# A transformer block with 32 experts: tokens 64 to 96 of an expert in banks of their own, the rarer rest at the end, the first expert without a branch

## The chip, the cores and the metric

The kernel runs on one core of one Trainium2 chip. The metric is device time in microseconds (us) from launch to end. Before the change it is 1229.9 us, the median of three runs (1229.08 to 1230.4).

Names: PE is the matrix engine, PEld its weight loads, DVE the vector engine, ACT the scalar engine, POOL GpSimd, SP the engine that issues the weight transfers. An engine's sequencer, which takes its branches and register loads, has the same name with a q behind it (PEq; PEldq in listings by line).

## The reference

x has 256 tokens of 1024 features. Attention and its merge come first; the change does not touch them. Behind them a router picks 4 of 32 experts for each token, and the experts are added up:

```python
def moe_ffn(h, w_router, b_router, w_gate_up, b_gate_up, w_down, b_down):
    hf = h.reshape(b * s, d)
    logits = (hf @ w_router + b_router).astype(jnp.float32)
    top_val, top_idx = lax.top_k(logits, TOP_K)            # TOP_K = 4
    top_w = jax.nn.softmax(top_val, axis=-1)
    combine = jnp.sum(jax.nn.one_hot(top_idx, N_EXPERTS) * top_w[..., None], axis=1)
    y = jnp.zeros_like(hf)
    for e in range(N_EXPERTS):                             # 32
        gu = hf @ w_gate_up[e] + b_gate_up[e]              # 1024 -> 2048
        gate = jnp.minimum(gu[:, :D_EXPERT], SWIGLU_LIMIT)
        up = jnp.clip(gu[:, D_EXPERT:], -SWIGLU_LIMIT, SWIGLU_LIMIT)
        act = (up + 1.0) * (gate * jax.nn.sigmoid(SWIGLU_ALPHA * gate))
        y = y + combine[:, e:e + 1] * (act @ w_down[e] + b_down[e])   # 1024 -> 1024
```

The result goes through an RMS norm, a gate and the residual: `x + gt_f * rms_norm(ffn_out, g_post_ffn)`. All is float32, so an expert has 12.58 MB of weights.

## The kernel before

The first 240 us or so are the mixing part and the router. Then the expert phase runs over all 32 experts in order, and all weights of all experts are read once.

**The weight stream.** An expert's weights are six pieces of 2 MB: four quarters of `w_gate_up[e]` and two halves of `w_down[e]`. `Slots.pump` (L76) puts them on SP's queue in one fixed order, the halves of `w_down[e-1]` behind the quarters of `w_gate_up[e]`. Ten slots of the on-chip memory take turns. The transfer into a slot waits until PE has read the piece that lay there.

**A step.** Step j multiplies the up product of expert j and the down product of expert j−1. A gather (L922, `gather_quad`, every fourth step, for four experts) collects the first 64 tokens of an expert as columns. The up product (`up_mm`, L959) is 64 matmuls of 64 rows by 512 columns into two banks, `ps_g`. ACT and DVE copy one bank each to memory (`up_out`, L972 and L970). Then come, on PE, on odd steps the scatter of the two experts before (`add_pair`, L1072, 8 matmuls into the four banks `y`) and the rows for the next scatter (L1061), and on all steps two times 16 matmuls of `down(j-1)` (L1026), each half followed by four transposes of the copied up product (`up_act`, L979). DVE and ACT add the biases, clip and apply the sigmoid to the transposes (L986 to L998), and take the down product out of its bank (`down`, L1048 on ACT and L1049 on DVE).

**The arms.** An expert can have more than 64 tokens. `counts` (L875 to L883) counts the tokens of each expert and writes a number `arm[j]` per step. Each step begins with `more(j)`: all engines load `arm[j]` (L1132) and branch (L1133) over code that does tokens 64 to 96, 96 to 128, 128 to 192 and 192 to 256 (`CHUNKS`) of expert j−1 (down, `more_down`) and expert j (up, `more_up`). The up product of an arm uses the same two banks `ps_g`. `hint(j)` tells PE beforehand where the branch will go. In these inputs expert 11 alone has over 64 tokens, and not over 96: its arm runs ahead of step 11 (up) and ahead of step 12 (down).

**The order around the branches.** A scheduler sorts each engine's instructions by their data; code of an arm and code outside do not mix, so that an instruction stands ahead of a branch or behind it. `add_pair` had no place of its own: one of its matmuls stands ahead of the odd step's up product, seven behind it. `more(E)`, the branch after the last step, covers the arm of expert 31. Behind it comes the end: the broadcast of a row by PE (`ps_bc`, L292), the rest of `down(31)`, the last scatter, the norm's root, which ACT forms by two functions (L227 and L228) for each half of the tokens, the last DVE operation (L1214) with the residual x, which SP reloads (L1204), and the write of the output. `preload_act_table_set(EXP_LN)` (L1198) loads ACT's function table for the root ahead of that branch.

## Time and profile before

| what | us |
|---|---|
| median of three runs | 1229.9 (1229.08 to 1230.4) |
| the profiled execution | 1233.0 |
| its span, first to last instruction | 1231.3 |
| PE busy in the span | 1090.5 (89%) |
| DVE busy | 441.0 (36%) |
| ACT busy | 247.5 (20%) |
| weight queue, share of the 16 DMA engines | 90.5%, 459.87 MB |
| mean granted PE clock | 0.943 |

All sums are made within the profiled execution, so against its span of 1231.3 us and not against the median. PE and the DMA engines are both near 90% on the average of the span. An average can't say which of them limits a stretch, so stretches are read one by one below. In a timeline the bracket at the end of a row is the idle time of the engine before the row's instruction and what ended it. DMA share 1.00 means that all 16 engines were busy all the time.

### The profile page before, as it was taken

The page shows a single profiled execution, that of the slowest core. Times are in us where ns is not written, and L with a number is a line of the kernel's source. Part 1 is how long each engine was busy: PE and PEld are TensorE (multiplying, and loading weights), DVE is VectorE, ACT ScalarE, POOL GpSimd, SP SyncE. Part 2 cuts the span into 40 slices and gives each one's busy share as a digit, 9 for nine tenths or more (in the row PEclk, how much of TensorE's full clock was granted, in tenths as well). Part 3 has the DMA queues.
Part 4 walks back from the last instruction along what each step waited for, and adds up shares of the span by engine and source line. Part 5 has one row for each costly group of instructions (what it writes and reads, how often), then busy time and mean ns, then how long its engine had stood idle before and what let it go on. Part 6 is the DMA issues. An engine that isn't in the chain of part 4 may idle for free. (4 is left out here: it accounts for less than half of the span.)

```text
span 1231.3 us, 14468 instructions
## 1 busy us (share of the span) xinstructions
PE 1090.5 (89%) x5655; PEld 543.4 (44%) x5655; DVE 441.0 (36%) x952; ACT 247.5 (20%) x473; POOL 30.3 (2%) x44
## 2 busy tenths in 40 slices
PE   4999999688798898998979998998998989989997
PEld 3987899533243334334333333334333423343333
DVE  2587977522222323222132223223233232232224
ACT  2355774520011101001110011101101110010013
POOL 2022000200000000000000000000000000000000
PEclk9999999788899989888989999999999999999999
DMA  9978796768999999999559999999999999999992
GB/s 301 392 273 332 285 402 260 306 257 337 426 374 385 426 426 426 422 426 427 237 228 419 424 426 428 424 426 427 426 425 427 424 426 427 426 426 427 425 397 96
DMA packets 52357, 464.09 MB, mean 377 GB/s; under 512 B 4149, under 2 KB 4266, under 8 KB 27498
## 3 DMA queue, kind: packets, MB, share of 16 engines
q1 hardware_dynamic: 51274, 459.87, 90.5%
q8 instruction: 85, 1.39, 0.5%
q0 software_dynamic: 352, 0.67, 0.4%
q10 hardware_dynamic: 576, 1.57, 0.3%
q14 instruction: 70, 0.57, 0.1%
HBM read 460.01 MB, written 2.10 MB: 375 GB/s over the span
## 5 line engine op out<-in xcount | busy, mean ns | idle before, releaser
L959 PE MATMUL ps_g<-w,xe 128*64 128x512 f32 (+1 forms) x2112 | 501.0, 642 | 76.1 <-ACTq L1133 59.7
L959 PEld LDWEIGHTS ps_g<-w,xe 128*64 128x64 f32 (+1 forms) x2112 | 168.2, 146 | 387.7 <-issue 308.6
L1026 PE MATMUL ps_d<-w,act 128*64 128x512 f32 x992 | 226.0, 597 | 2.2 <-ACT xe L903 2.2
L970 DVE COPY gu<-ps_g 128x512 f32<-128x512 f32 x32 | 22.1, 692 | 438.5 <-PE ps_g L959 438.5
L1026 PEld LDWEIGHTS ps_d<-w,act 128*64 128x64 f32 x992 | 69.0, 137 | 121.8 <-issue 112.8
L972 ACT COPY gu<-ps_g 128x512 f32<-128x512 f32 x33 | 19.3, 585 | 492.1 <-PE ps_g L959 492.1
L463 PE MATMUL ps_p<-hT,whi 128*128 128x256 f32 x512 | 97.0, 290 | 3.2 <-ACT whi L412 3.2
L986 DVE TENSOR_TENSOR gate<-ps_t,bcol 128x256 f32<-128x256 f32 x64 | 27.2, 424 | 165.1 <-PE ps_t L979 116.0
L463 PEld LDWEIGHTS ps_p<-hT,whi 128*128 128x128 f32 x512 | 80.5, 194 | 6.7 <-ACT whi L412 3.5
L413 DVE TENSOR_TENSOR wlo<-w,whi 128x1024 fp32r<-128x1024 f32 x56 | 68.5, 1227 | 29.9 <-ACT whi L412 29.4
L463 PE MATMUL ps_p<-hT,wlo 128*128 128x256 f32 x256 | 72.8, 288 | 0.3 <-DVE wlo L413 0.2
L995 ACT ACTIVATE act<-gate 128x256 f32<-128x256 f32 x64 | 26.6, 416 | 219.1 <-DVE gate L994 219.1
L412 ACT CAST whi<-w 128x1024 fp32r<-128x1024 f32 x56 | 58.5, 1047 | 58.6 <-PE ps_p L463 27.9
L979 PEld LDWEIGHTS ps_t<-ident,gu 128*128 128x128 f32 x260 | 36.3, 209 | 53.1 <-issue 50.3
L1048 ACT ACTIVATE dn<-ps_d,wsl 64x512 fp32r<-64x512 f32 x62 | 42.3, 682 | 82.6 <-PE ps_d L1026 67.0
L922 PE MATMUL ps_x<-p,xn 128*128 128x256 f32 (+1 forms) x288 | 43.1, 304 | 10.7 <-DVE cf L880 4.4
L463 PEld LDWEIGHTS ps_p<-hT,wlo 128*128 128x128 f32 x256 | 49.0, 193 | 1.7 <-DVE wlo L413 1.4
L979 PE MATMUL ps_t<-ident,gu 128*128 128x128 f32 x260 | 48.7, 310 | 0.9 <-ACT gu L972 0.8
L1072 PE MATMUL y<-dn,st 128*128 128x512 f32 x128 | 38.1, 420 | 12.4 <-PEq L1133 9.5
L922 PEld LDWEIGHTS ps_x<-p,xn 128*128 128x128 f32 x288 | 40.9, 218 | 14.5 <-issue 6.2
L1049 DVE SCALAR_TENSOR_TENSOR dn<-ps_d,wsl,dn 64x512 fp32r<-64x512 f32 x62 | 46.4, 748 | 1.5
L1072 PEld LDWEIGHTS y<-dn,st 128*128 128x128 f32 x128 | 22.8, 188 | 31.9 <-issue 22.1
(248 smaller groups left out, 777.3 us busy)
## 6 DMA issues: line engine op xcount, KB each, us to landing
w<-in_w_gate_up_dram SPq DMA_DIRECT2D x128, 2048.0 KB, 18.5
w<-in_w_down_dram SPq DMA_DIRECT2D x62, 2048.0 KB, 16.2
w<-in_w_in_dram SPq DMA_DIRECT2D x8, 2048.0 KB, 8.0
w<-in_w_mod_dram SPq DMA_DIRECT2D x8, 2048.0 KB, 10.1
w<-in_w_mod_dram SPq DMA_DIRECT2D x4, 1024.0 KB, 8.6
w<-in_w_mod_dram SPq DMA_DIRECT2D x8, 512.0 KB
w<-in_w_in_dram SPq DMA_DIRECT2D x8, 512.0 KB, 11.5
w<-in_w_out_dram SPq DMA_DIRECT2D x2, 2048.0 KB
```

Source lines behind the costliest of these rows:

```text
L412: nc.scalar.copy(hi, w)
L413: nc.vector.tensor_tensor(lo, w, hi.bitcast(FT), op=OP.subtract)
L463: mm(ps[:, f % 2, :], w[:, kk, f * 128:(f + 1) * 128], hT[:, a, k, :], start=(k == 0 and i == 0 and f % 2 == 0), stop=(k == NK - 1 and i = ...
L922: mm(px[:, j, :], xn[:, t, a, feature(k0 + j)], p[:, t].rearrange("p a b -> p (a b)"), start=(t == 0 and a == 0), stop=(t == 1 and a == 1))
L959: last = mm(pg[b][s * C:(s + 1) * C, :], xe[:, k, :], wt[:, k % 2, c0:c0 + 512], start=(k == 0), stop=(k == NK - 1), skip_group_check=True)
L979: nc.tensor.transpose(pt[:, j, :], gu[:, j:j + 509:4], ident)
L986: nc.vector.tensor_tensor(dst, pt[:, :, 64 * m:64 * m + 64], bcol[:, b0 + 4 * b:b0 + 4 * b + 4, None].to_broadcast([128, 4, 64]), op=OP.add)
L995: state_act["sig"] = nc.scalar.activation(sig, gate, AF.Sigmoid, scale=1.702)
L1026: mm(pds[h][p0:p0 + C, :], a, wt[:, k % 4, h * 512:(h + 1) * 512], start=(k == 0), stop=(k == NK - 1), skip_group_check=True)
L1048: state_act["down"] = nc.scalar.activation(hi, pds[h][rows, :], AF.Copy, scale=weight)
L1049: nc.vector.scalar_tensor_tensor(lo, pds[h][rows, :], weight, hi.bitcast(FT), op0=OP.mult, op1=OP.subtract)
L1072: mm(yps[t][h], sts[p][:, h, t * 128:(t + 1) * 128], dns[p][:, h, a, :], start=False, stop=False, skip_group_check=True)
```

## The change

- The arms in the steps do tokens 64 to 96 only. Their up product goes to a bank `ps_go` of the pool that the transposes use. A dummy transpose into each of the two banks `ps_g` (L1118) at the beginning of the arm makes PE the engine that last used them.
- Tokens from 96 on (for expert 0: from 64 on) are done behind the last step, in `more(E)`, by `rest`, chunk by chunk under branches on a new table `cnt`, with weights that POOL reloads into the slots (`Slots.again`). `arm[E]` holds 4 more when one of them is needed.
- `more(0)` is gone. `counts` stands behind the first up product instead of ahead of the first gather.
- `add_pair` is placed behind the end of the up product.
- The hint for the last branch goes to ACT and DVE too.
- The preload of ACT's table is tied to the last down and sigmoid ahead of `more(E)`.
- The zero fill `aov` and the copies of activations to memory (`aov_far`) are gone.

```diff
@@ -79,6 +79,11 @@
     def data(self, name, slot, shape, dt=FT):
         assert self.ready(name, slot), name
         return self.pools[slot].tile(shape, dt, name=name, tag=f"w{slot}")
+
+    def again(self, i, slot):
+        src, shape, _, _ = self.items[i]
+        self.tiles[i] = self.pools[slot].tile([128] + list(shape), FT, name=f"w{slot}", tag=f"w{slot}")
+        self.nc.gpsimd.dma_start(self.tiles[i], src)
 
     def done(self, *names):
         self.gone.update(names)
@@ -207,6 +212,7 @@
     comb = keep.tile([128, 2, E], FT, name="comb")
     rank = keep.tile([128, 2, E], FT, name="rank")
     arm = keep.tile([1, E + 1], I32, name="arm")
+    cnt = keep.tile([1, E], I32, name="cnt")
     rs = keep.tile([128, 2], FT, name="rs")
     m8 = keep.tile([128, 2, 8], FT, name="m8")
     oh = keep.tile([128, 2, TOPK, E], FT, name="oh")
@@ -857,8 +863,6 @@
     mk = ctx.enter_context(tc.tile_pool(name="moe", bufs=1, side="right"))
     wk = ctx.enter_context(tc.tile_pool(name="ework", bufs=1, side="right"))
     aov = mk.tile([128, 256], FT, name="aov")
-    nc.gpsimd.memset(aov, 0.0)
-    aov_far = dram.tile([128, 1280], FT, name="aov_far")
     rp = mk
     bd = wk.tile([2 * E, 512], FT, name="bd", tag="st_e")
     for h in range(2):
@@ -870,17 +874,21 @@
 
     def counts():
 
+
         pn = pst.tile([1, E], FT, name="ps_n", tag="t")
         for t in range(2):
             mm(pn, ones[:, 0:1], msk[:, t, :], start=(t == 0), stop=(t == 1))
-        cf = wk.tile([1, 2, E + 2], FT, name="cf", tag="so")
-        cm = wk.tile([1, 2, E + 1], FT, name="cm", tag="pwt")
+        cf = wk.tile([1, 3, E + 2], FT, name="cf", tag="so")
         nc.vector.memset(cf, 0.0)
-        nc.vector.tensor_scalar(cf[:, 0, 1:E + 1], pn, 64.0, None, op0=OP.is_gt)
-        nc.vector.tensor_scalar(cf[:, 1, 1:E + 1], pn, 96.0, 3.0, op0=OP.is_gt, op1=OP.mult)
-        nc.vector.scalar_tensor_tensor(cm[:, 0, :], cf[:, 0, 0:E + 1], 2.0, cf[:, 0, 1:E + 2], op0=OP.mult, op1=OP.add)
-        nc.vector.tensor_tensor(cm[:, 1, :], cf[:, 1, 0:E + 1], cf[:, 1, 1:E + 2], op=OP.max)
-        nc.vector.tensor_tensor(arm, cm[:, 0, :], cm[:, 1, :], op=OP.max)
+        nc.vector.tensor_copy(cnt, pn)
+        nc.vector.tensor_scalar(cf[:, 0, 2:E + 1], pn[:, 1:E], 64.0, None, op0=OP.is_gt)
+        nc.vector.scalar_tensor_tensor(cf[:, 1, 0:E + 1], cf[:, 0, 0:E + 1], 2.0, cf[:, 0, 1:E + 2], op0=OP.mult,
+                                       op1=OP.add)
+        nc.vector.tensor_scalar(cf[:, 2, 0:1], pn[:, 0:1], 64.0, 4.0, op0=OP.is_gt, op1=OP.mult)
+        nc.vector.tensor_scalar(cf[:, 2, 1:E], pn[:, 1:E], 96.0, 4.0, op0=OP.is_gt, op1=OP.mult)
+        nc.vector.tensor_reduce(cf[:, 2, E:E + 1], cf[:, 2, 0:E], AX.X, OP.max)
+        nc.vector.tensor_tensor(cf[:, 1, E:E + 1], cf[:, 1, E:E + 1], cf[:, 2, E:E + 1], op=OP.add)
+        nc.vector.tensor_copy(arm, cf[:, 1, 0:E + 1])
 
     def weights():
 
@@ -960,6 +968,7 @@
                               start=(k == 0), stop=(k == NK - 1), skip_group_check=True)
                     if k == ks[0]:
                         state_act["up"] = last
+                    state_act["up_end"] = last
             if release and k % 2:
                 W.done(i_gu[e][k // 2])
         return pg
@@ -967,9 +976,9 @@
     def up_out(pg, b, tag, bufs):
         gu = wk.tile([128, 512], FT, name="gu", tag=tag, bufs=bufs)
         if b % 2:
-            nc.vector.tensor_copy(gu, pg[b])
+            state_act["evac_dve"] = nc.vector.tensor_copy(gu, pg[b])
         else:
-            nc.scalar.copy(gu, pg[b])
+            state_act["evac_act"] = nc.scalar.copy(gu, pg[b])
         return gu
 
     def up_act(e, C, b, gu, act):
@@ -1097,52 +1106,62 @@
                 mm(yps[t][h], ct[h * E:(h + 1) * E, t * 128:(t + 1) * 128], bd[h * E:(h + 1) * E, :], start=True,
                    stop=False, skip_group_check=True)
 
-    def chunk_act(i, write):
+    ov = aov.rearrange("p (j m) -> p j m", m=64)
+
+    def more_down(e):
+        s0, C = CHUNKS[0]
+        scatter(down_32(e, ov, "guo"), scatter_rows(e, s0, "so", C))
+
+    def more_up(e):
+        s0, C = CHUNKS[0]
+        for bank in gu_banks():
+            nc.tensor.transpose(bank[:, :128], ident, ident)
+        xo = gather([e], s0, C, "xo")[:, :, 0, :]
+        pg = up_mm(e, C, xo, pg=[pst.tile([128, 512], FT, name="ps_go", tag="t")])
+        up_act(e, C, 0, up_out(pg, 0, "guo", 1), ov)
+
+    def load(t, j):
+        return nc.values_load(t[0:1, j:j + 1], engines=ENGINES, min_val=0, max_val=S)
+
+    def rest(e, i):
+
         s0, C = CHUNKS[i]
...
+        with tc.If(load(cnt, e) > s0):
+            if i == (e > 0):
+                for q in range(4):
+                    W.again(i_gu[e][q], redo_slots[q])
+                for q in range(2):
+                    W.again(i_dn[e][q], redo_slots[4 + q])
+            pg = up_mm(e, C, gather([e], s0, C, "xo")[:, :, 0, :])
+            a = wk.tile([128, C // 8, 64], FT, name="ao", tag="xo")
+            for b in range(C // 32):
+                up_act(e, C, b, up_out(pg, b, "guo", 1), a)
+            st = scatter_rows(e, s0, "so", C)
+            scatter(down_64(e, a) if C == 64 else down_32(e, a, "guo"), st)
+            if i + 1 < len(CHUNKS):
+                rest(e, i + 1)
 
     def hint(j):
 
-        tc.mark_branch_hint_location(f"more{j}", "LikelyTaken", [mybir.EngineType.PE])
+        tc.mark_branch_hint_location(f"more{j}", "LikelyTaken", ENGINES[:3] if j == E else ENGINES[:1])
 
     def more(j):
 
-        at = nc.values_load(arm[0:1, j:j + 1], engines=ENGINES, min_val=0, max_val=3)
+
+        at = load(arm, j)
         with tc.If(at > 0, label=f"more{j}"):
-            if j:
-                with tc.If(at > 1):
-                    more_down(j - 1, 0)
+            if j > 1:
+                with tc.If((at != 4) if j == E else (at > 1)):
+                    more_down(j - 1)
             if j < E:
                 with tc.If(at != 2):
-                    more_up(j, 0)
-            with tc.If(at > 2):
-                for i in range(1, len(CHUNKS)):
-                    if j:
-                        more_down(j - 1, i)
-                    if j < E:
-                        more_up(j, i)
+                    more_up(j)
+            else:
+                with tc.If(at > 3):
+                    streamed = dict(W.tiles)
+                    for e in range(E):
+                        rest(e, int(e > 0))
+                    W.tiles = streamed
 
     redo_slots = [W.items[k][2] for k in i_gu[E - 1] + i_dn[E - 3]]
     quads, gus, acts, sts, wsl, dns = {}, {}, {}, {}, {}, {}
@@ -1155,17 +1174,13 @@
             acts[j] = wk.tile([128, 8, 64], FT, name="act", tag="act", bufs=2)
         up_act(j, 64, b, gus[j][b], acts[j])
 
+    pgs = []
+
     def first_up(xe, ks):
         if ks[0] == 0:
-            more(0)
             pgs[:] = gu_banks()
         up_mm(0, 64, xe[:, :, 0, :], True, pgs, ks)
 
-    pgs = []
-
-    with tc.issue_after(state_act["route"].ins):
-        hint(0)
-    counts()
     for j in range(E):
         if j == 0:
             gather_quad(0, first_up)
@@ -1175,14 +1190,18 @@
             more(j)
         xe = quads[j // 4][:, :, j % 4, :]
         pg = up_mm(j, 64, xe, True) if j else up_mm(0, 64, xe, True, pgs, range(NK - 2, NK))
-        with tc.issue_after(state_act["up"].ins):
+        gus[j] = [up_out(pg, b, "gu", 2) for b in range(2)]
+        with ExitStack() as stack:
+            for name in ("up", "evac_act", "evac_dve")[:3 if j + 1 == E else 1]:
+                stack.enter_context(tc.issue_after(state_act[name].ins))
             hint(j + 1)
-        gus[j] = [up_out(pg, b, "gu", 2) for b in range(2)]
         if j % 2 and j >= 3:
-            add_pair((j - 3) // 2)
+            with tc.issue_after(state_act["up_end"].ins):
+                add_pair((j - 3) // 2)
         if j % 4 == 3 and j < E - 1:
             gather_quad(j + 1)
         if j == 0:
+            counts()
             weights()
         elif j % 2:
             scatter_pair(j - 1)
@@ -1191,10 +1210,11 @@
         else:
             for b in range(2):
                 activate(0, b)
+    before = state_act["down"], state_act["sig"]
     more(E)
     gtf = wk.tile([128, 2, 512], FT, name="gtf", tag="xe")
     bcast_row([gtf[:, h, :] for h in range(2)], ggf, pst, "t", nc.scalar.copy)
-    with tc.issue_after(state_act["down"].ins), tc.issue_after(state_act["sig"].ins):
+    with tc.issue_after(before[0].ins), tc.issue_after(before[1].ins):
         nc.scalar.preload_act_table_set(EXP_LN)
     down(E - 1)
     add_pair((E - 1) // 2)
```

Left out: one hunk in which the router's matmul no longer leaves its handle `route`.

**Start of an up product on PE, before.** An even step; rows ahead are the last transposes in the arm's code, and `L1133` is the end of the branch. `Activation_49` and `DVE_49` are ACT's and DVE's counters that PE waits for.

```order
4804 L979 MATMUL ps_t_15497<-ident_106,gu_15495 128x128 [waits DVE_49]
4805 L979 MATMUL ps_t_15497<-ident_106,gu_15495 128x128 x3
4806 L1140 UNCONDITIONAL_BRANCH
4807 L1140 UNCONDITIONAL_BRANCH [waits PE_49]
4808 L1133 UNCONDITIONAL_BRANCH [waits PE_49]
4809 L959 MATMUL ps_g_15512<-w0_14181,xe_13468 64x512 [waits DMAHW0_49,PE_49,Activation_49]
4810 L959 MATMUL ps_g_15512<-w0_14181,xe_13468 64x512
4811 L959 MATMUL ps_g_15513<-w0_14181,xe_13468 64x512 [waits DVE_49,PE_49]
4812 L959 MATMUL ps_g_15513<-w0_14181,xe_13468 64x512
```

The same place after:

```order
2379 L988 MATMUL ps_t_7452<-ident_106,gu_7450 128x128 [waits Activation_49]
2380 L988 MATMUL ps_t_7452<-ident_106,gu_7450 128x128 x3
2381 L1157 UNCONDITIONAL_BRANCH
2382 L1157 UNCONDITIONAL_BRANCH [waits PE_49]
2383 L1152 UNCONDITIONAL_BRANCH [waits PE_49]
2384 L967 MATMUL ps_g_7466<-w0_6977,xe_6685 64x512 [waits DMAHW0_49,PE_49]
2385 L967 MATMUL ps_g_7466<-w0_6977,xe_6685 64x512
2386 L967 MATMUL ps_g_7467<-w0_6977,xe_6685 64x512 [waits PE_49]
2387 L967 MATMUL ps_g_7467<-w0_6977,xe_6685 64x512
```

The first matmul of each of the two banks no longer waits for ACT and DVE; it waits for the weights (`DMAHW0_49`) and for PE itself.

**The last step and the end on PE, before.** `w_23832` and `w_23842` are the halves of down(30), `w_23852` and `w_23863` those of down(31); an `x2` row here is the first quarter of the latter's eight matmuls; between the two parts stands the arm's code.

```order
3333 L1026 MATMUL ps_d<-w_23842,act 64x512 x8
3334 L979 MATMUL ps_t<-ident,gu 128x128 x4
3335 L1026 MATMUL ps_g<-w_23852,act 64x512 x8
3336 L1026 MATMUL ps_g<-w_23863,act 64x512 x2
3337 L1133 COMPARE_AND_BRANCH
...
3370 L1133 UNCONDITIONAL_BRANCH
3371 L292 MATMUL ps_bc<-ident,ggf 128x128 x8
3372 L1026 MATMUL ps_g<-w_23863,act 64x512 x6
3373 L1072 MATMUL y_2578<-dn_24599,st_24549 128x512
```

After, the halves are `w_10734` and `w_10744`, and `w_10754` and `w_10765`; between the parts stands `rest` for all experts:

```order
1941 L1035 MATMUL ps_d<-w_10734,act 64x512 x8
1942 L988 MATMUL ps_t<-ident,gu 128x128 x4
1943 L1035 MATMUL ps_d<-w_10744,act 64x512 x8
1944 L988 MATMUL ps_t<-ident,gu 128x128 x4
1945 L1152 COMPARE_AND_BRANCH
...
3573 L1152 UNCONDITIONAL_BRANCH
3574 L298 MATMUL ps_bc<-ident,ggf 128x128 x8
3575 L1035 MATMUL ps_g<-w_10754,act 64x512 x8
3576 L1035 MATMUL ps_g<-w_10765,act 64x512 x8
3577 L1081 MATMUL y_2577<-dn_11082,st_11032 128x512
```

All matmuls of down(31) have moved from ahead of the last branch to behind it, and behind the row broadcast `ps_bc`.

**The root at the end on ACT, before.** L227 and L228 are the two functions, once for each half of the tokens; the table was loaded ahead of the branch.

```order
1183 L226 ACTIVATE rb<-sso,eps 128x1
1184 L1209 ACTIVATE fin,sso<-y_2581 128x512
1185 L227 ACTIVATE rz_r<-sso,rb 128x1
1186 L226 ACTIVATE rb<-sso,eps 128x1
1187 L228 ACTIVATE rz_r<-rz_r 128x1
1188 L227 ACTIVATE rz_r<-sso,rb 128x1
1189 L228 ACTIVATE rz_r<-rz_r 128x1
```

After (the same lines are L232, L233 and L234):

```order
1433 L232 ACTIVATE rb<-sso,eps 128x1
1434 L1229 ACTIVATE fin,sso<-y_2580 128x512
1435 L233 ACT_TABLE_LOAD
1436 L233 ACTIVATE rz_r<-sso,rb 128x1
1437 L232 ACTIVATE rb<-sso,eps 128x1
1438 L234 ACT_TABLE_LOAD
1439 L234 ACTIVATE rz_r<-rz_r 128x1
1440 L233 ACT_TABLE_LOAD
1441 L233 ACTIVATE rz_r<-sso,rb 128x1
1442 L234 ACT_TABLE_LOAD
1443 L234 ACTIVATE rz_r<-rz_r 128x1
```

Four table loads have come in, one ahead of each of the four operations of L233 and L234.

## Rows read from the trace of the kernel before

**Rows 1.** Stretches of the expert phase: us, busy per engine, PEclk, DMA share, GB/s

```profile
278.00:286.00 8.00, 7.48 (x30) 2.71 (x32) 1.43 (x6) 0.00 (x0) 0.00 (x0) 0.79 0.32 88
365.00:383.00 18.00, 14.92 (x66) 5.59 (x64) 5.33 (x14) 2.20 (x4) 0.00 (x0) 0.91 0.85 309
586.00:606.00 20.00, 18.14 (x107) 6.07 (x101) 3.44 (x12) 1.32 (x3) 0.00 (x0) 0.94 0.36 132
622.00:650.00 28.00, 21.85 (x108) 8.09 (x108) 6.63 (x17) 2.57 (x5) 0.00 (x0) 0.88 0.55 200
650.00:1194.00 544.00, 492.56 (x2211) 193.83 (x2208) 152.90 (x385) 61.87 (x111) 0.00 (x0) 0.96 1.01 426
1206.00:1216.00 10.00, 9.93 (x48) 3.52 (x44) 5.33 (x14) 3.48 (x5) 0.00 (x0) 1.00 0.07 29
```

**Rows 2.** Waits of the whole program: us in total, times, longest us

```profile
PE ps_g L959 <- ACTq L1133: 59.7, 25, 2.7
...
PE ps_g L959 <- PEq L1133: 11.0, 3, 4.8
```

**Rows 3.** Timeline of PE, 1040 to 1188: start, us, what, [idle before <-releaser]

```profile
1043.55 14.09 PE L959 MATMUL ps_g<-w,xe 128*64 128x512 f32 x64 [2.71 <-ACTq L1133]
...
1066.17 0.47 PE L1072 MATMUL y<-dn,st 128*128 128x512 f32 x1 [0.15 <-PEq L1133]
1068.82 15.84 PE L959 MATMUL ps_g<-w,xe 128*64 128x512 f32 x64 [2.18 <-ACTq L1133]
...
1159.55 14.14 PE L959 MATMUL ps_g<-w,xe 128*64 128x512 f32 x64 [2.66 <-ACTq L1133]
```

**Rows 4.** DMA issues of the page: count, KB each, us to landing

```profile
w<-in_w_gate_up_dram SPq DMA_DIRECT2D x128, 2048.0 KB, 18.5
...
x<-x_far SPq DMA_DIRECT2D x1, 1024.0 KB, 17.5
```

**Rows 5.** Stretches of two up products; columns as in the first group

```profile
1043.50:1057.60 14.10, 14.05 (x66) 5.59 (x68) 0.81 (x2) 0.58 (x1) 0.00 (x0) 1.00 1.00 423
1068.80:1084.60 15.80, 15.71 (x65) 5.22 (x65) 2.36 (x8) 0.58 (x1) 0.00 (x0) 0.89 1.01 430
```

**Rows 6.** Timeline of PE around the arm of expert 11

```profile
572.89 0.75 PE L979 MATMUL ps_t<-ident,gu 128*128 128x128 f32 x4
...
595.62 0.50 PE L1072 MATMUL y<-dn,st 128*128 128x512 f32 x1 [0.44 <-PEq L1140]
...
618.41 3.65 PE L1026 MATMUL ps_d<-w,act 128*64 128x512 f32 x16 [0.30 <-ACT xe L903]
```

**Rows 7.** PE after the start; loads of 320:345 and branches: ns min/median/max

```profile
250.07 5.59 PE L959 MATMUL ps_g<-w,xe 128*64 128x512 f32 x16 [1.40 <-ACTq L1133]
...
278.52 3.74 PE L959 MATMUL ps_g<-w,xe 128*64 128x512 f32 x10 [4.77 <-PEq L1133]
...
L1132 PEldq TENSOR_LOAD <-arm x17: 295/299/313, 326.4 to 337.6; - x17
...
L1133 PEldq COMPARE_BRANCH  x33: 74/345/6216, 248.0 to 1214.3; - x33
```

**Rows 8.** Timeline of all engines at the end, 1205 to 1232

```profile
1211.42 4.51 PE L1026 MATMUL ps_g<-w,act 128*64 128x512 f32 x20
...
1214.08 1.28 ACT L1198 ACT_TABLE_LOAD   x1
...
1216.24 1.06 PE L292 MATMUL ps_bc<-ident,ggf 128*128 128x128 f32 x8 [0.31 <-PEq L1133]
...
1225.37 2.73 DVE L1214 SCALAR_TENSOR_TENSOR fin<-fin,rz_r,x 128x512 f32<-128x512 f32 x4
1225.45 0.20 ACT L228 ACTIVATE rz_r<-rz_r 128x1 f32<-128x1 f32 x1
```

**Rows 9.** The page: its first line

```profile
span 1231.3 us, 14468 instructions
```

**Rows 10.** Groups by form: count, busy us, mean ns, idle before

```profile
L959 PE MATMUL ps_g<-w,xe 128*64 128x512 f32 x2048 | 492.1, 640 | 76.1 <-ACTq L1133 59.7 <-PEq L1133 11.0 <-DMA w<-in_w_gate_up_dram 3.1
```

More of the change, by code (lines that the diff above doesn't have):

```diff
@@ L791, in route_mm @@
             for s in range(4):
-                state_act["route"] = mm(pqs[t][32 * s:32 * s + 32, :], wra[:, 4 * h + s, :], xTs[t, h][:, s, :],
-                                        start=(h == 0), stop=(h == 1), skip_group_check=True)
+                mm(pqs[t][32 * s:32 * s + 32, :], wra[:, 4 * h + s, :], xTs[t, h][:, s, :], start=(h == 0),
+                   stop=(h == 1), skip_group_check=True)
         def route_top(t):
@@ L1098, in scatter_bias @@
                    stop=False, skip_group_check=True)
-    def chunk_act(i, write):
-        s0, C = CHUNKS[i]
-        if i == 0:
-            return aov.rearrange("p (j m) -> p j m", m=64), None
-        a = wk.tile([128, C // 8, 64], FT, name="ao", tag="xo")
-        far = aov_far[:, (s0 - 96) * 8:(s0 - 96 + C) * 8].rearrange("p (j m) -> p j m", m=64)
-        if not write:
-            nc.gpsimd.dma_start(a, far)
-        return a, far
-    def more_down(e, i):
-        s0, C = CHUNKS[i]
-        a = chunk_act(i, False)[0]
-        st = scatter_rows(e, s0, "so", C)
-        scatter(down_64(e, a) if C == 64 else down_32(e, a, "guo"), st)
@@ L1116, in more_up @@
-    def more_up(e, i):
-        s0, C = CHUNKS[i]
-        xo = gather([e], s0, C, "xo")[:, :, 0, :]
-        pg = up_mm(e, C, xo)
-        a, far = chunk_act(i, True)
-        for b in range(C // 32):
-            up_act(e, C, b, up_out(pg, b, "guo", 1), a)
-        if far is not None:
-            nc.gpsimd.dma_start(far, a)
+    ov = aov.rearrange("p (j m) -> p j m", m=64)
+    def more_down(e):
+        s0, C = CHUNKS[0]
+        scatter(down_32(e, ov, "guo"), scatter_rows(e, s0, "so", C))
```

## The prediction

> **What bounds the kernel now.** I began with the stretches of the expert phase, because they show where the weight stream stood still [rows 1]. From 650 to 1194 us the DMA engines move 426 GB/s at a share of 1.01: there the stream is the limit. It falls to 88 GB/s at 278–286, to 309 at 365–383, to 132 at 586–606 and to 200 at 622–650. Length times (1 − rate/426) is the time lost: 6.3, 4.9, 13.8 and 14.9 us. The last two lie where the arm of expert 11 runs, the only one that this data opens. So 28.7 us are lost at the arm, and 11.2 in the two stretches after the start.
>
> The waits say why [rows 2]. A transfer is issued when PE has released its slot, so a standstill means that PE was late. Ahead of the up product PE idles 59.7 us in 25 waits for ACT's sequencer at the branch, 2.4 each, and 11.0 us in 3 for its own. The timeline shows such steps [rows 3]: an up product of 14.09 us after 2.71 us idle; and, an expert later, one matmul of the pair scatter 0.15 us after PE's branch, and then 2.18 us of waiting before the up product. So passing the branch costs PE some 0.15 to 0.3 us; the rest is that ACT and DVE free the up product's banks only when they are past the branch themselves. Four experts, from 1043.55 to 1159.55, take 116.0 us, 29.0 each. An expert's six pieces of 2.097 MB [rows 4] take 6 × 4.92 = 29.5 us at 426 GB/s. PE runs half a microsecond per expert ahead of the stream, and so can't make up a delay.
>
> **The change, part by part.**
>
> *Banks of their own.* The first matmuls behind the branch no longer wait for ACT and DVE. Per expert 2.4 us go, of which I leave 0.3 for the branch: 2.1. Besides, some up products ran at a lower granted clock: 0.89 (of 2.4 GHz) in the stretch from 1068.8, with 15.71 us of matmuls, against 1.00 and 14.05 from 1043.5 [rows 5]. Where that goes with the pauses, 1.7 us on half of the experts, 0.8 on the mean. PE then needs 29.0 − 2.1 = 26.9, at best 26.1 us. In the steady stretch this is worth nothing, as the stream takes 29.5 and the weights are late next. It is worth a lead of 2.6 to 3.4 us per expert.
>
> *The arm of expert 11.* From the transposes before it (572.89 + 0.75) to the first matmul behind it (595.62) PE spends 22.0 us [rows 6]. The new arm does the same work in another bank, two transposes more (0.19 each, from 0.75 for four) being 0.4. The standstills were 28.7 us long although PE had gained 0.5 per expert. Now each of the nine experts from 2 to 10 gains 2.1 to 2.9 more, 19 to 26, and the arm's two branches lose 2.4 twice: 24 to 31 of the 28.7. The gain lies between 15 (half of the lead gone by the start) and 28.7; I take 28.7, the end that the sum is nearer to.
>
> *The start.* The first expert's branch goes, for which PE waited 1.40 us [rows 7]. Ahead of the third expert's, PE's sequencer made 17 loads of counts from 326.4 to 337.6, 0.70 us apart; the order now has 14, so 2.1 less. At 278.52 the 4.77 us are the sequencer's, in a branch; of 33 branches the median took 0.345 us and the longest 6.216. Whether this one stays slow is not to be seen: from nothing to all of it, and I take half, 2.4. Sum 5.9, from 2 to 10.
>
> *The slowest DMA engine.* From 1206 to 1216 the stream moves 29 GB/s at a share of 0.07 [rows 1]: one engine of sixteen is about 10 us behind the others, 560 us after the last standstill, in which it caught up: 1.8%. Without the standstills its lag of the 240 us before them is not swallowed: +4.3 us. Bounds 0 (the lag doesn't recur) and +10.
>
> The last weights landed before 1216, which I put at 1214. After: 1214 − 28.7 − 5.9 + 4.3 = 1183.7.
>
> *The end.* Before, the transposes of the last step were done when the twenty matmuls of down(31) began, at 1211.4 [rows 8], and the span ended 19.9 us later, at 1231.3 [rows 9]. After, PE follows the stream: the second half of down(30) lands two pieces, 9.8 us, before the last one, and 3.65 of matmuls and 0.75 of transposes follow [rows 6]: 1183.7 − 9.8 + 4.4 = 1178.3. The work behind grows [rows 8]:
> - The twenty matmuls, 4.51 us, stood ahead of the branch, beside the last work of DVE and ACT. They are behind it now, and PE's work there still begins with ps_bc (1216.24), 4.8 us after the transposes, because that waits for DVE and ACT. +4.5; nothing only if PE need not wait.
> - ACT loads a table for each change between the two functions of the root, two loads per half of the tokens, four in a chain at 1.28 us. Before, the second factor was ready at 1225.45 + 0.20 and DVE's last 2.73 us began at 1225.37. After, the second factor is 5.1 later against those, at 1230.8 on that scale, and half of DVE's work, 1.37, follows it: 1232.1 instead of 1228.1. +4.0; at least 2.6, if only two loads count.
> - PE begins again after 4.8 us of idling. The first sixteen matmuls of the phase took 5.59 us [rows 7], sixteen later ones 3.65 [rows 6]. Up to 1.9, at least 0; I take 1.2.
> - The reload of x is issued behind the branch. It took 17.5 us to land behind weights [rows 4]; L1214, which needs it, would begin some 21 us after the transposes. Hidden: nothing; 2 at most.
>
> The Trainium skill (ScalarE: Activation LUTs, What ACT_TABLE_LOAD costs) puts a switch at about 2.66 us, a drain of 1.38 included. The row here has 1.28 and shows no drain. By the page the four would cost 5.5 us more, an estimate, and the time would be 1212.
>
> The tail is 19.9 + 4.5 + 4.0 + 1.2 = 29.6, and the span 1178.3 + 29.6 = 1207.9, 23.4 under the 1231.3. The profiled execution took 1233.0 us, 1.7 beside its span and 3.1 over the median; the gain taken from the median of 1229.9 gives 1206.5, so 1207.
>
> **Rivals.**
>
> *A, the forecast:* the stream sets the end, and the tail gives back a quarter. 1207, own range 1196 to 1218. Chance 0.60.
>
> *B, more.* The lag does not grow (−4.3), the start gains 10 (−4.1), PE stays warm (−1.2), only two table loads count (−1.4): 1207 − 11 = 1196; with down(31) hidden as well 1191. For it stands the share of 1.01 over 544 us; against it the 29 GB/s at the end. 0.14.
>
> *C, slower: the fetch behind the branch takes the place of the wait.* PE jumps over the arm at each expert. If the target is not there, the sequencer waits up to 6.2 us [rows 7], part of which lay hidden behind ACT's wait. It decides from the point where most of the 31 branches cost 2.2 us again: PE stays near 29.0 per expert, the 28.7 of the arm stay, the start gains 4, the tail still grows by 9.7: 1229.9 + 5.7 = 1236. Against it: PE's sequencer ended only 3 waits of the up product [rows 2], and the matmul at 1066.17 came 0.15 us behind the branch [rows 3]. 0.11.
>
> *D, the lead is too short.* Half of the arm's standstill stays, 14.3, and 3 of the start: 1207 + 17 = 1224. If all but some 12 us of it stays, the tail eats the rest and nothing changes. 0.15 together, 0.05 of it for no change.
>
> The Trainium skill (Runtime: NRT & Kernel Launch, Instruction fetch mechanics) says that a taken branch to a target outside the loaded pages forces a fetch. That is C's rule and speaks against this change, above all at the last branch, behind which all chunks of all experts now stand. The trace agrees in a few branches (6.2 us) and not in the median one (0.345 us). If the last one alone missed, the time would be 1207 + 6 = 1213, inside A.
>
> That the code for more than 96 tokens runs is excluded: the up product of 64 rows ran 2048 times [rows 10], 32 × 64, so no larger chunk was computed.
>
> **How the numbers follow.** About 0.2%, 2.5 us, can be told from no change here. Faster: A 0.60, B 0.14 and the first part of D 0.10, together 0.84. Same 0.05, slower 0.11 (C). Out of the range stay C, the end of D and the lowest of B: 1189 to 1225.
>
> **What would show it.** PE's waits of the up product for ACT are gone, and waits for DMA on w stand in their place; the rate stays at 426 from 350 to about 1180 without the dips at the arm; one engine works on for 10 us or more at the end; the last transposes end near 1178, ps_bc follows after 4.8; ACT has four table loads between its last small operations, and the span ends 29 to 30 us after the transposes. I am wrong if the dips at the arm stay, if the up product waits for the sequencer at most branches, or if the tail is under 25 us.

## The result, and the profile after

The changed kernel takes 1195.1 us, the median of 4 runs (1193.1 to 1195.9); the kernel before took 1230.15 us beside it. The ratio is 0.9712, 95% interval 0.9696 to 0.9729, so 33 to 37 us less. Forecast were 1207 us. The range and the direction hold; the gain is half as large again as the 23 us of the sum.

The page's first lines of the changed kernel, with the granted clock and the rate in 40 slices of the span:

```profile
span 1193.7 us, 14305 instructions
...
PE 1057.3 (89%) x5657; PEld 546.3 (46%) x5657; DVE 442.1 (37%) x955; ACT 253.0 (21%) x477; POOL 30.1 (3%) x43
...
PEclk9999999988999999997999999999999999999997
...
GB/s 290 391 286 329 303 378 272 377 227 367 427 406 405 427 426 425 427 426 427 428 425 427 426 427 425 427 429 424 428 425 427 428 426 427 427 426 426 428 365 51
```

The span before is in [rows 9]. The rate has no dip in the middle any more. In the clock row, from the eleventh slice on (298 us), one slice alone before the last is under 9: that of 537 to 567 us, where the arm runs. The same stretches as in [rows 1], where the weights came to a stop before:

```profile
258.00:278.00 20.00, 18.37 (x76) 6.69 (x74) 6.98 (x28) 2.70 (x4) 0.00 (x0) 0.83 0.81 315
278.00:286.00 8.00, 8.00 (x40) 2.79 (x37) 0.15 (x1) 0.58 (x1) 0.00 (x0) 1.00 0.99 420
343.00:365.00 22.00, 20.84 (x110) 11.18 (x108) 10.06 (x23) 5.04 (x9) 0.00 (x0) 1.00 0.95 382
365.00:383.00 18.00, 18.00 (x86) 6.98 (x82) 2.70 (x7) 1.00 (x2) 0.00 (x0) 1.00 1.00 422
586.00:606.00 20.00, 18.03 (x100) 6.93 (x98) 4.62 (x11) 2.15 (x4) 0.00 (x0) 1.00 1.00 426
622.00:650.00 28.00, 27.70 (x132) 11.67 (x130) 8.74 (x23) 2.78 (x5) 0.00 (x0) 1.00 1.01 426
650.00:1150.00 500.00, 437.65 (x2039) 177.66 (x2036) 138.65 (x348) 56.91 (x102) 0.00 (x0) 1.00 1.01 426
```

From 383 to about 1150 the stream runs at 426 GB/s; both standstills at the arm are gone. Where PE waits now (us in total, times, longest), against [rows 2]:

```profile
PE ps_g L967 <- DMA w<-in_w_gate_up_dram: 44.0, 39, 1.6
...
PE ps_g L967 <- PEq L1152: 16.2, 22, 7.1
...
PE ps_d L1035 <- DMA w<-in_w_down_dram: 12.3, 15, 1.3
...
PE ps_bc L298 <- DVEq L1152: 8.4, 1, 8.4
```

The 59.7 us behind ACT's sequencer have no row any more. In their place are 44.0 us of waiting for weights of the up product and 12.3 for the down product. The sequencer's own 16.2 us are 22 waits, most of 0.30 us; the two long ones are the loads of counts ahead of steps 2 and 3. PE's timeline at the start:

```profile
245.62 4.51 PE L967 MATMUL ps_g<-w,xe 128*64 128x512 f32 x16
...
269.11 16.70 PE L967 MATMUL ps_g<-w,xe 128*64 128x512 f32 x64 [0.30 <-PEq L1152]
...
329.06 11.34 PE L967 MATMUL ps_g<-w,xe 128*64 128x512 f32 x42 [7.10 <-PEq L1152]
```

And late in the phase, up to the last transposes:

```profile
1139.29 3.65 PE L967 MATMUL ps_g<-w,xe 128*64 128x512 f32 x16 [1.25 <-DMA w<-in_w_gate_up_dram]
1144.19 3.65 PE L967 MATMUL ps_g<-w,xe 128*64 128x512 f32 x16 [1.25 <-DMA w<-in_w_gate_up_dram]
...
1155.03 3.65 PE L1035 MATMUL ps_d<-w,act 128*64 128x512 f32 x16 [0.31 <-DMA w<-in_w_down_dram]
1158.62 0.75 PE L988 MATMUL ps_t<-ident,gu 128*128 128x128 f32 x4
```

The first up product begins at 245.62 and no more at 250.07, the second expert's at 269.11 and no more at 278.52 [rows 7]. Late in the phase PE waits 1.25 us ahead of each quarter of weights and takes one every 4.90 us: the stream sets the pace. The last transposes end at 1159.37.

The end, all engines, against [rows 8]:

```profile
1162.11 0.76 DVE L1058 SCALAR_TENSOR_TENSOR dn<-ps_d,wsl,dn 64x512 fp32r<-64x512 f32 x1
1165.42 1.28 ACT L299 ACT_TABLE_LOAD   x1 [2.19 <-ACTq L1152]
...
1167.79 1.94 PE L298 MATMUL ps_bc<-ident,ggf 128*128 128x128 f32 x8 [8.42 <-DVEq L1152]
...
1169.66 8.42 PE L1035 MATMUL ps_g<-w,act 128*64 128x512 f32 x32
...
1182.80 1.28 ACT L233 ACT_TABLE_LOAD   x1
1184.10 0.29 ACT L233 ACTIVATE rz_r<-sso,rb 128x1 f32<-128x1 f32 x1
...
1189.01 0.20 ACT L234 ACTIVATE rz_r<-rz_r 128x1 f32<-128x1 f32 x1
1189.25 1.41 DVE L1234 SCALAR_TENSOR_TENSOR fin<-fin,rz_r,x 128x512 f32<-128x512 f32 x2 [1.71 <-ACT rz_r L234]
```

The table load at 1182.80 is the first of the chain of four loads; the activation behind it begins at 1184.10. The span ends 34.3 us after the last transposes, against 19.9 before. So the transposes came 52.1 us earlier, and the end gave 14.4 of it back.

### The profile page after: what moved, and what is told of

It is laid out like the page before. It is cut to its first block, busy times and chain, and to the rows that moved or that the text cites. A ratio compares the mean times of both kernels' runs of the same rounds, so it can differ in the third digit from the quotient of the medians.

```text
span 1193.7 us, 14305 instructions
## 1 busy us (share of the span) xinstructions
PE 1057.3 (89%) x5657; PEld 546.3 (46%) x5657; DVE 442.1 (37%) x955; ACT 253.0 (21%) x477; POOL 30.1 (3%) x43
## 5 line engine op out<-in xcount | busy, mean ns | idle before, releaser
L967 PE MATMUL ps_g<-w,xe 128*64 128x512 f32 x2048 | 462.3, 603 | 61.9 <-DMA w<-in_w_gate_up_dram 44.0
L967 PEld LDWEIGHTS ps_g<-w,xe 128*64 128x64 f32 x2048 | 168.2, 138 | 334.1 <-issue 227.8
L1035 PE MATMUL ps_d<-w,act 128*64 128x512 f32 x992 | 226.6, 597 | 14.5 <-DMA w<-in_w_down_dram 12.3
L264 DVE SCALAR_TENSOR_TENSOR mod_acc<-w,sg,mod_acc 128x1024 f32<-128x1024 f32 x28 | 36.3, 1296 | 0.2
L913 DVE TENSOR_SCALAR xe<-ps_x,af,modc 128x256 f32<-128x256 f32 (+1 forms) x36 | 18.6, 518 | 46.4 <-PE ps_x L930 46.1
## 6 DMA issues: line engine op xcount, KB each, us to landing
w<-in_w_in_dram SPq DMA_DIRECT2D x8, 512.0 KB, 12.3
```

The costliest lines, as they stand in the source:

```text
L264: nc.vector.scalar_tensor_tensor(self.acc, wt, sg[:, k:k + 1], self.acc, op0=OP.mult, op1=OP.add)
L967: last = mm(pg[b][s * C:(s + 1) * C, :], xe[:, k, :], wt[:, k % 2, c0:c0 + 512], start=(k == 0), stop=(k == NK - 1), skip_group_check=True)
L1035: mm(pds[h][p0:p0 + C, :], a, wt[:, k % 4, h * 512:(h + 1) * 512], start=(k == 0), stop=(k == NK - 1), skip_group_check=True)
```

## Experiments

Each ratio is to the kernel before on the same chip; the changed kernel has 0.9712. The kernel before has medians from 1230.15 to 1232.44 us on these chips, so a difference between the medians of two versions can be off by some 2 us; where not said otherwise, a difference is that of the ratios, times 1230 us. Landing times of single parts of a transfer, below, are read from the traces.

### Is it the wait for ACT and DVE?

**One bank only.** The arm's up product back in a bank of the up product:

```diff
-        for bank in gu_banks():
-            nc.tensor.transpose(bank[:, :128], ident, ident)
-        pg = up_mm(e, C, xo, pg=[pst.tile([128, 512], FT, name="ps_go", tag="t")])
+        pg = up_mm(e, C, xo)
```

> The changed kernel with one part undone: the arm's up product is in the bank ps_g again, without the two dummy transposes. Theory (the lead): the first matmul behind each branch waits for ACT again, about 2 us in each of some 28 steps, PE falls back to 28 us or more per expert, has hardly a lead over the stream's 29.5, and most of the standstill at the arm returns: rate well under 400 GB/s somewhere between 530 and 620 us, 1210 to 1220 us. Rival (the wait never mattered, since the stream sets the pace, and the gain came from the start and the shorter arm): 1193 to 1198 us, no dip at the arm.

Measured 1206.5 us, 0.9799 (0.9766 to 0.9832). That fits neither the theory nor the rival, and it settles nothing. The arm then uses one bank of two, so the scheduler put the 32 matmuls of the other bank ahead of the branch; no wait of PE for ACT is in its profile. It was no undoing of the change. Why it costs 11 us I did not take apart.

**Both banks.** The arm writes both banks again, and ACT and DVE each read one:

```diff
-        pg = up_mm(e, C, xo, pg=[pst.tile([128, 512], FT, name="ps_go", tag="t")])
+        pg = up_mm(e, C, xo, pg=gu_banks())
+        nc.tensor.transpose(pg[1][:, :128], ident, ident)
+        nc.vector.tensor_copy(scratch, pg[1][:, :128])
```

(The two dummy transposes at the arm's beginning are out; `scratch` is a tile that the arm has anyway.)

> The changed kernel with both banks of the up product used in the arm again: its up product is in the first bank, which ACT reads, and a transpose goes to the second, which DVE reads; so behind each branch PE's first two matmuls wait for ACT and DVE as in the kernel before. All else is the changed kernel. Theory (the lead): 2.2 to 2.7 us of waiting per step for ACT return and with them the lower clock in part of the up products; PE needs 28 to 29 us per expert, the stream stands still at the arm, 1210 to 1220 us. Rival (the shorter arm and the earlier start suffice for the lead): under 1202 us and no dip at the arm. The earlier run with the arm's up product in one bank only did not settle this, since half of the up product moved ahead of the branch there.

Measured 1224.3 us, 0.9943 (0.9921 to 0.9965). Its waits of the up product, columns as above:

```profile
PE ps_g L967 <- ACTq L1153: 65.9, 24, 2.9
```

And its stretches at the arm and behind it, columns as in [rows 1]:

```profile
570.00:586.00 16.00, 15.23 (x100) 5.05 (x94) 3.35 (x12) 1.00 (x2) 0.00 (x0) 1.00 0.62 244
606.00:622.00 16.00, 14.04 (x82) 5.59 (x82) 4.62 (x11) 2.15 (x4) 0.00 (x0) 1.00 0.68 249
650.00:1140.00 490.00, 439.54 (x1994) 168.96 (x1992) 137.55 (x343) 56.37 (x101) 0.00 (x0) 0.96 1.01 427
```

With the wait come back the standstill at the arm (244 and 249 GB/s) and a clock of 0.96 in the long stretch. So 28 us of the 35 hang on the banks (0.9943 − 0.9712 = 2.3% of 1230; 24 to 33 by the ends of the two intervals), more than the theory's 15 to 25. All other parts together leave 7 us, and the longer end is within these. The 28 us are not the 28.7 of the two standstills before, though: the two rows above lose 6.8 and 6.6 us, 13.4 in all. The rest is lead: PE ends its last transposes at 1186.2, 9 us behind the last part of the weights (1177.0), where in the changed kernel they end 5.5 us ahead of it (1159.4 and 1164.9).

**Without the arm.** The threshold of the arm at 96 tokens, in the kernel before and in the changed one:

```diff
-  ... pn, 64.0, None, op0=OP.is_gt)
+  ... pn, 96.0, None, op0=OP.is_gt)
```

> The kernel before, with the arms' threshold at 96 in place of 64, so that expert 11's arm is never entered; it leaves out the tokens from 64 on of expert 11. Theory (the two standstills are the arm's whole price): 28.7 us less than before, 1198 to 1204 us. Rival (PE sets the pace throughout, so that all of the arm's PE time of some 37 us goes): 1190 to 1195 us. If the standstills had another cause: 1225 or more.

> The changed kernel with the threshold at 96, so that expert 11's arm is never entered; it leaves out the tokens from 64 on of expert 11. Theory (the lead covers the arm and the stream sets the pace): no change, 1193 to 1197 us. Rival (PE still sets the pace): the arm's PE time, some 24 to 30 us, goes: 1165 to 1172 us.

Before without the arm: 1207.9 us, 0.9805 (0.9784 to 0.9827), so 21 to 27 us less, a little under the 28.7 of the standstills; the time lies outside the theory's range, 4 us above its end. Changed without the arm: 1194.9 us, 0.9704 (0.9683 to 0.9725), no change. The arm that cost 24 us is free once PE has a lead. What before_no_arm lacks of its gain is not PE's lateness at the end, for there PE waits for weights:

```profile
1177.72 3.65 PE L959 MATMUL ps_g<-w,xe 128*64 128x512 f32 x16 [1.25 <-DMA w<-in_w_gate_up_dram]
```

In its trace (the slowest of the five executions) the last part of the weights lands at 1197.6, 15.4 us after the other fifteen; in the kernel before the last is 10.6 behind. So the slowest DMA engine can account for 4.8 us; that it does is not shown.

### The start

**Counting ahead of the gather again** (`counts()` in front of the loop):

> The changed kernel with the counting placed ahead of the first gather again, still without a branch for the first expert. Theory (before, DVE's zero fill of the counts' tile waited 2.5 us for POOL and held up the first gather; the stream then carries every late microsecond at its start to the end): the first up product starts about 3 us later, near 248.6, and the time is 2.5 to 3.5 us longer, about 1198. Rival (only the branch held up the first up product): within 1 us of the changed kernel.

Measured 1200.2 us, 0.9742 (0.9722 to 0.9762), 3.7 us more by the ratios, whose intervals just overlap, and 5.0 between the medians. The size is near the theory's, its place is not: the first up product began at 246.91, only 1.3 later, and DVE's zero fill waited for nothing. Most of the rest is lost at the branch of step 3, where PE waited 7.10 us in the changed kernel:

```profile
332.45 4.50 PE L967 MATMUL ps_g<-w,xe 128*64 128x512 f32 x9 [9.12 <-PEq L1152]
```

From 330 to 350 us the stream loses some 4 us there and 0.5 in the changed kernel (estimated from the bytes moved, against 426 GB/s). Why this branch took longer is open.

**POOL's zero fill.** In the kernel before, POOL filled `aov` between its operations on `xn`, the tokens that the gather reads. POOL's timeline there:

```profile
241.50 0.31 POOL L860 MEMSET aov<- 128x256 f32 x1 [3.69 <-DMA x_far<-xt]
241.77 2.48 POOL L846 TENSOR_TENSOR xn<-whole,xn 128x512 fp32r<-128x512 f32 x2
```

And DVE's:

```profile
244.31 0.12 DVE L878 MEMSET cf<- 1x68 f32 x1 [2.48 <-POOL xn L846]
244.36 0.35 DVE L913 TENSOR_TENSOR p<-iota,rank 128x256 fp32r<-128x256 f32 x1
```

The fill takes 0.31 us but waited 3.69 for the copy of x to memory; the next two operations on `xn` stood behind it, and DVE and the gather behind them. The change has no fill. Put back:

```diff
     aov = mk.tile([128, 256], FT, name="aov")
+    nc.gpsimd.memset(aov, 0.0)
```

> The changed kernel with POOL's zero fill of the arm's activations put back ahead of its last two operations on xn. Theory (before, this fill waited 3.7 us for the copy of x to memory and held up POOL's xn, which the first gather and DVE's zero fill wait for): the first up product starts 2.5 to 3.5 us later than 245.6 and the time is 2.5 to 3.5 us longer, some 1198. Rival (the fill costs its own 0.3 us): no change, within 1 us.

POOL's fill in that kernel's timeline:

```profile
242.73 0.31 POOL L866 MEMSET aov<- 128x256 f32 x1 [5.30 <-DMA x_far<-xt]
```

On PE:

```profile
249.50 3.65 PE L968 MATMUL ps_g<-w,xe 128*64 128x512 f32 x16
```

The first up product is 3.9 us later, so it is shown that the fill holds it up. Of the time only a part is left: 1197.1 us, 0.9726 (0.9696 to 0.9757); the interval includes none and all of it. The first issue of the stream (253.19) is 3.0 us later and the last transposes are 2.7 us later.

### The end

**Without the code behind the last step** (`rest` and its branch are out):

> The changed kernel without the code for more than 96 tokens behind the last step (in these inputs no expert needs it). Theory (the longer end is this code's: 20 matmuls of down(31) back ahead of the branch 4.5 us, the late branch of DVE and ACT 3.6, the colder PE 2, the table loads 4.3): the last transposes stay near 1159.5, the span ends 20 to 21 us behind them, 1180 to 1184 us. Rival (DVE and ACT are late at the last branch whatever stands behind it): 1184 to 1188 us.

Measured 1180.1 us, 0.9591 (0.9552 to 0.9631). PE's rows at the end:

```profile
1157.80 0.75 PE L988 MATMUL ps_t<-ident,gu 128*128 128x128 f32 x4
1158.48 4.51 PE L1035 MATMUL ps_g<-w,act 128*64 128x512 f32 x20
1163.35 1.06 PE L298 MATMUL ps_bc<-ident,ggf 128*128 128x128 f32 x8 [0.36 <-PEq L1152]
```

Twenty matmuls of down(31) stand ahead of the branch, PE waits 0.36 us behind it where it waited 8.42, and the span ends 19.9 us after the transposes (1178.4 − 1158.5), as in the kernel before. The whole longer end is due to this code's being there, although none of it runs.

**The table load behind the last branch:**

```diff
-    with tc.issue_after(before[0].ins), tc.issue_after(before[1].ins):
-        nc.scalar.preload_act_table_set(EXP_LN)
     down(E - 1)
+    with tc.issue_after(state_act["down"].ins):
+        nc.scalar.preload_act_table_set(EXP_LN)
```

> The changed kernel with ACT's table load for the root placed behind down(31)'s last operation on ACT, behind the last branch; all else unchanged. Theory (each table load on the chain costs its 1.28 us and no more): one load in place of four on the chain, beside PE's last scatter, 4.0 to 4.4 us less, 1190 to 1192 us. Rival (a load drains the engine besides, 2.66 us each): 6 us or more less, below 1189.5. Rival (the loads lie beside DVE's work): 1194 or more.

Measured 1190.75 us, 0.9662 (0.9646 to 0.9678), 4.4 us less between the medians and 6 by the ratios. The next two runs, on the same chip as this one, change nothing and took 4.3 and 3.7 us more. The last matmuls of down(31) in its timeline:

```profile
1168.50 8.89 PE L1035 MATMUL ps_g<-w,act 128*64 128x512 f32 x32
```

From their end, 1177.4, to the end of the span, 1189.5, are 12.1 us; in the changed kernel they are 15.6. So the loads' own share is 3.5 us: four loads on the chain became one, partly beside PE's scatter. The 6 us or more of the rival with a drain are not in the trace.

**No hint for ACT and DVE at the last branch** (`ENGINES[:1]` for all j):

> The changed kernel without the hints for the last branch on ACT and DVE (PE keeps its own). Theory (the hint doesn't save these two the fetch, which still took 3 to 5 us): no change, 1194 to 1197 us. Rival (the hint saves part of it): 2 us longer or more.

Measured 1195.0 us, 0.9698 (0.9682 to 0.9714). PE still waits 8.03 us for DVE:

```profile
1167.34 1.94 PE L298 MATMUL ps_bc<-ident,ggf 128*128 128x128 f32 x8 [8.03 <-DVEq L1152]
```

The hint to these two saves nothing that can be measured.

**The pair scatter where the scheduler puts it** (`issue_after(up_end)` out):

> The changed kernel with the pair scatter free to stand where the scheduler puts it, so ahead of the up product in part. Theory (the stream sets the pace, so PE's order within a step is worth nothing): 1193.5 to 1197 us. Rival (it keeps PE from the up product for some 2 us at every other branch, and with that from the lead that the arm needs): 1198 or more.

Measured 1194.5 us, 0.9692 (0.9674 to 0.971): no difference, as the stream sets the pace.

**All of the last step ahead of the branch.** The order is now down(31), its scatter, the broadcast, then `more(E)`, with one table load behind:

```diff
-    before = state_act["down"], state_act["sig"]
-    more(E)
     bcast_row([gtf[:, h, :] for h in range(2)], ggf, pst, "t", nc.scalar.copy)
-    with tc.issue_after(before[0].ins), tc.issue_after(before[1].ins):
-        nc.scalar.preload_act_table_set(EXP_LN)
     down(E - 1)
     add_pair((E - 1) // 2)
+    more(E)
...
+            if t == h == 0:
+                with tc.issue_after(square.ins):
+                    nc.scalar.preload_act_table_set(EXP_LN)
```

> The changed kernel with down(31), its scatter and the row broadcast ahead of the last branch, and one table load behind it; the code for more than 96 tokens stays. Theory: the late branch of ACT and DVE (4 to 5 us) stays but lies partly beside PE's last scatter; no wait of PE for it, one table load in place of four: 1182 to 1187 us. Rival (the fetch behind the last branch is simply moved to the end of the chain): 1188 to 1192 us.

Measured 1184.1 us, 0.9615 (0.9584 to 0.9647). DVE's last operation waited there for x, whose reload SP issued behind the branch:

```profile
1172.73 0.33 SPq L1220 DMA_DIRECT2D x<-x_far  x1
...
1174.86 2.81 DVE L1229 TENSOR_TENSOR fin<-y,gtf 128x512 f32<-128x512 f32 x4 [3.20 <-DVEq L1152]
...
1179.12 2.74 DVE L1233 SCALAR_TENSOR_TENSOR fin<-fin,rz_r,x 128x512 f32<-128x512 f32 x4 [1.45 <-DMA x<-x_far]
```

So the reload was put ahead of it as well, into the slot of down(30)'s first half:

```diff
+    x_slot = W.items[i_dn[E - 2][0]][2]
+    x1 = W.pools[x_slot].tile([128, 2, D], FT, name="x1", tag=f"w{x_slot}")
+    nc.sync.dma_start(x1, x1_far)
     more(E)
```

> The kernel with down(31), its scatter and the broadcast ahead of the last branch and one table load behind it, and now the reload of x ahead of that branch too, into the slot of down(30)'s first half; the code for more than 96 tokens stays. Theory (there, DVE's last operation waited 1.45 us for x): 1.3 to 1.6 us less than with x behind the branch, 1181 to 1184 us. Rival (the reload takes time from the last weights): no gain or a loss of up to 2 us.

The first line of its page, and DVE's last operation in its timeline, which waits for nothing now:

```profile
span 1180.6 us, 14302 instructions
```

Timeline:

```profile
1174.68 2.73 DVE L1234 SCALAR_TENSOR_TENSOR fin<-fin,rz_r,x 128x512 f32<-128x512 f32 x4
```

Measured 1182.7 us, 0.9604 (0.9587 to 0.9621). The wait for x is gone, and the step of 1.4 us is as large as expected, though the two intervals overlap. This is the fastest version that keeps the code for more than 96 tokens: 12 us under the changed kernel, 49 under the one before.

## Why the prediction was right in kind and short in size

**Banks, lead, arm: right.** The waits for ACT went, waits for weights came, and the arm became free. The gain of 28.7 us, taken at the upper end, is borne out by the stretches, which show no standstill at the arm any more; that undoing the banks costs as much (arm_waits, 28 us) is in part chance, as only 13.4 of it are standstills. Rival C is refuted: behind most branches PE waits 0.30 us, so no wait of its sequencer takes the old wait's place. The Trainium skill (Runtime: NRT & Kernel Launch, Instruction fetch mechanics) warns of a fetch at each taken branch out of the loaded pages. PE's traces show a long wait at few branches; the delay of ACT and DVE at the last one fits the warning, but no run shows the fetch itself.

**The clock: right.** From 650 to 1150 the granted clock is 1.00, and sixteen matmuls take 3.65 us, where before some up products had 0.89 [rows 5]. PE idles 1.25 us ahead of a quarter now, and the clock stays; with the pauses of 2.7 us back (arm_waits) it is 0.96 again.

**The last weights: right before the change, 18.8 us too late after it.** The trace keeps 16 landing times for each transfer, one for each DMA engine. Of the last weights before, fifteen parts landed from 1197.3 to 1203.6 and the sixteenth at 1214.2, which is the 1214 of the prediction. After, the last part landed at 1164.9 instead of 1183.7. The step behind that holds: the transposes end 5.5 us ahead of the last weights, where the prediction has 9.8 − 4.4 = 5.4, so they too came some 19 us early, at 1159.4 instead of 1178.3.

**The slowest DMA engine, +4.3: the step that failed.** What the prediction read in the kernel before is right: the 29 GB/s at 1206 to 1216 [rows 1] are one engine with late weights (a sixteenth of 426 is 26.6). Its sixteenth of x, which stands behind these weights, landed at 1217.0, and the others' by 1206.1. The lag also built up as it says: first and last part of a transfer landed 0.9 us apart at 657 and 15.6 at 1117. But it did not grow by the change. Of the last weights after, seven parts landed from 1151.8 to 1156.2 and nine from 1163.3 to 1164.9, and the stream's share shows engines without work from 1152 on:

```profile
1152.00:1154.00 2.00, 2.00 (x11) 0.55 (x7) 0.00 (x0) 0.00 (x0) 0.00 (x0) 1.00 0.70 295
1158.00:1160.00 2.00, 1.37 (x8) 0.56 (x4) 0.60 (x2) 0.68 (x1) 0.00 (x0) 1.00 0.57 229
```

The last part came 12.5 us behind the mean of the sixteen before and 5.7 after: −6.8 in place of +4.3, so 11 of the 19 us. Why the lag shrank is open. It is 15.1 us in before_no_arm and 3.5 to 6.6 in every version of the changed kernel, on three chips, so it goes with the code and not with a chip. In the profile's pages the packets of one instruction queue (count, MB, share of the engines) halved, which may or may not be the reason; before:

```profile
q14 instruction: 70, 0.57, 0.1%
```

After:

```profile
q14 instruction: 36, 0.29, 0.1%
```

**The start, −5.9: too small.** Of its terms, the loads of counts are as forecast: the wait ahead of step 3 went from 9.16 to 7.10 us, 2.1 less. The slow branch ahead of the second expert went wholly (4.77 to 0.30 us) and not by half. And the first issue came 5.5 us earlier instead of 1.4, because POOL's fill, an edit that I did not price at all, had held up the gather: with the fill back it is 3.0 us later. The remaining 2.5 hold the 1.4 for the branch. With 16 us of standstills in the start before (11 in [rows 1], some 5 around them) and some 10 after, the start gave about 11.6 us. This is 6 of the 19; about 2 have no place.

**The end, +9.7: too small.** It grew by 14.4. The twenty matmuls (4.5) and the table loads (4.3, from the last matmul of down(31) to the end: 15.6 us after, 11.3 before) are as forecast. The start of ps_bc came 8.42 us after the transposes and not 4.8 (+3.6): DVE's last operation ended at 1162.87, and DVE let PE go at 1167.7. This delay of DVE goes when the skipped code goes (no_rest), and fits the fetch behind the last branch that I had priced at 6 us beside rival C and left out of the sum. The colder PE (granted clock 0.50 from 1166 to 1170, the level of 1.2 GHz) cost 2.0 instead of 1.2: ps_bc 1.94 for 1.06, 32 matmuls 8.42 for 7.30.

So two misses lie against each other, 19 us too late at the transposes and 4.7 too short behind them. The time of 1195.1 is a little under A's own range (1196 to 1218) and at B's 1196. Of B's four conditions two came true, the lag that does not grow and the larger gain in the start; the warm PE and the two table loads did not.

**The table loads' price.** The row is right: 1.28 each, and the next activation starts 0.02 us behind a load (1182.80 + 1.28 = 1184.08, then 1184.10). One load in place of four gave 3.5 us in the trace (table_late). The Trainium skill (ScalarE: Activation LUTs, What ACT_TABLE_LOAD costs) adds a drain of 1.38 to each; there is none in this chain.

Not settled: why the slowest engine lags less after the change, why the branch of step 3 takes longer with counting first, and what of POOL's 3.9 us arrives at the end.

## What to carry to other kernels

When a stream of weights and an engine are both near their limit, an engine's short waits cost nothing where they stand but take the lead that pays for a rare long job; look for who must pass a branch before a buffer is free, and give rare code buffers that one engine owns. A stream ends with its slowest DMA engine: read when each part of the last transfer landed, and don't carry a lag over to a changed kernel as if it were fixed. Code that is never entered was not free here: instructions that were ahead of a branch fell behind it, engines went on late there, and function tables were loaded anew.

## What the runs showed of the hardware that was not expected

- A hint ahead of the last branch did not spare ACT and DVE the late continuation: PE waited 8.4 us for DVE with it and 8.0 without, and 0.36 where the skipped code was short.
- A zero fill of 0.31 us on POOL delayed the first up product by 3.9 us, by the DMA that it waited for.
- One DMA engine of sixteen fell behind the others while the stream ran without a standstill: first and last part of a transfer landed 0.9 us apart at 657 and 15.6 at 1117 in the kernel before, and 13.1 at the end of the changed one.
- A reload of 1 MB behind the last weights landed after 17.5 us where one engine lagged (before), after 7.9 in the changed kernel, and after 4.9 when issued 9 us after the last weights had landed (arm_waits).
